# Retention's first state copies in their former order, attention's third group of values split ahead of weights, and the last values copied out of PSUM

## The chip, the core and the metric

The kernel runs on one core of one Trainium2 chip. The metric is the device time of one launch in microseconds (us), as the median of several runs. A core has five engines with queues of their own, each of which runs its instructions in order: TensorE (PE in the profile, with PEld for its weight loads), VectorE (DVE), ScalarE (ACT), GpSimd (POOL) and SyncE (SP, which here only issues transfers). [...]

## The reference

One decoder block on 1024 tokens of width 1024, in float32. Its first sub-layer feeds one normalised input `h` into two mixers whose outputs are gated and added; its second is an MLP.

```python
proj = h @ w_in                                   # q, k, v, gate of both mixers
# retention, 4 heads, 8 chunks of 128 tokens each
s = einsum('bhid,bhjd->bhij', qi, ki) * inner_decay
o = einsum('bhij,bhje->bhie', s, vi) + einsum('bhid,bhde->bhie', qi, state) * q_decay
state = state * chunk_decay + einsum('bhjd,bhje->bhde', ki * k_decay, vi)
# dilated attention, 3 groups (window, dilation) of 4 heads; each gives o and its log-denominator
p = softmax(q k / sqrt(128) + bias);  o = p v
att = einsum('gbhs,gbhsd->bshd', softmax(lse over groups), o_all)
merged = sigmoid(gate_a) * (silu(rg) * groupnorm(ro)) @ w_ret_out + sigmoid(gate_b) * att @ w_att_out
x = x + g1 * (merged @ w_o);   x = x + g2 * (relu(h2 @ w_ff1) ** 2 @ w_ff2)
```

## The kernel before

**Every float32 product is three matmuls.** An operand is split into a high part (`nc.scalar.copy`, ACT, rounding to the matmul's type) and a low part (`nc.vector.tensor_sub`, DVE). `mm3` (line 203) then adds weight-low times input-high (L207), weight-high times input-low (L209) and high times high (L211) in one PSUM bank. So each operand of a matmul costs an ACT instruction and a DVE instruction ahead of it, and TensorE reads both halves.

**The order is written by hand.** There is no scheduler: each engine gets its instructions in the order in which the Python code emits them. `Steps` runs a list of steps; each step has loads (weights of 512 KB into three `raw` buffers, from SP) and a body. The call `ahead(...)` (in other steps `args[0](...)`) inside a body splits the weights of the following steps and prepares their other loads at that place. `weave` and `weave_pv` mix two sources of matmuls on TensorE: a projection (`proj_gen`, eight rounds of six matmuls) and another piece of work; `at(gen, n, call)` calls a function after round `n` of a projection. Where several are nested, the inner one calls first.

**Retention** is done by `chunk(h, c, ...)` (line 706), 32 times; `g` is its number. In each chunk TensorE works at a gate projection (`rg`, tile of two banks), cut into pieces by `ks`, and between the pieces at:

- `kv{h}{c}{i}`, two products of `kh`, `kl` with the values, which update the running state: for `g == 0` ACT and DVE copy them into `sh`, `sl` (L734, L735: the split state) and ACT copies them into `st` (L742, L744); afterwards DVE folds them into `st` (L739);
- `s_kt(i)`: the score `sT` and the transposed key `kT` of chunk `i`. ACT copies (L666), DVE adds and multiplies (L667, L668), ACT and DVE split (L669, L670), and the key goes the same way into `kh`, `kl` (L679, L680);
- `o{h}{c}`: the query with the split state, then the score with the values. DVE takes its statistics (L768 to L770), POOL raises to a power (L771), and DVE writes `onm` (L774), which ends the use of that bank;
- `oT`: four transposes of the `onm` of the chunk before.

`jit_qk(i)` splits query and key of chunk `i`: a copy on ACT (L630) and a subtraction on POOL (L631), the latter with nothing else but the power of L771 on its queue. At the end of a chunk ACT and DVE split the state again (L758, L759). All these products are in one ring of four PSUM banks (`ps_s`), so a product waits for the last reader of the bank four allocations before it; the gate projection and the accumulators of attention have a second ring of two double banks (`ps_mm`). In chunk 1 `ahead(2)` splits the gate weights of chunk 2 (L197 on ACT, L198 on DVE) and multiplies one row block of the conditioning matrix (`mod_prep`, L461 and L463 on DVE).

**Attention** goes in two passes, `pair` 0 and 1, over two of the four heads of each group. For each of six combinations, `att_step` projects keys (`ak`) and computes the scores of the combination before. Then `cover_step` projects parts of the gates while the weights of the softmax and the products with the values are done. `pv` works through banks of probabilities: transposes to `pt` (L1434), a split to `pth` (ACT, L1438) and `ptl` (DVE, L1439), then three matmuls for each block, of `pth` with the low values `vl` (L1458), of `ptl` with the high values `vh` (L1459) and of `pth` with `vh` (L1460). `v_split(pair, g)` (line 1339) makes `vh` from the loaded values (two ACT copies, L1343) and leaves the low part in place of the loaded tile (two DVE subtractions, L1350). Its tiles come from a ring of eight in SBUF.

`pv_end` (line 1462) adds the accumulator `pv{pair}{g}{a}` to the sum of the groups. For group 2 and head `a = 0`, ACT copies the accumulator to SBUF (L1473) and DVE adds it from there (L1476); for `a = 1`, DVE adds it straight from PSUM. Then ACT and DVE split the sum into `ah`, `al` (L1481, L1482), which feed the output projection `ao` (`att_out_step`).

The third group of values of pair 0 is used in the first step of pair 1 (`att_step(1, 0)`), where the key projection `ak` is woven with `pv(0, 2)`; that of pair 1 in `gate_step`, which is woven with `pv(1, 1, 2)` and followed by `att_out_step`.

Of the kernel before, what the change touches and what calls it, by code (L numbers as in the profile page):

```python
# [17 lines left out]
P = 128  # L18
D = 1024
S = 1024  # L20
NK = D // P
# [119 lines left out]
def block_kernel(ctx, tc, io, stop=None, dbg=None):  # L141
    nc = tc.nc
# [354 lines left out]
    def at(gen, n, call):  # L497

        for i, _ in enumerate(gen):
            if i == n:  # L500
                call()
            yield
# [203 lines left out]
    def chunk(h, c, ahead, w=None):  # L706
        p = R["p"]
        g = NC * h + c
        if g + 3 < NG:
            fetch(g + 3)  # L710
        if c % 2 == 0:
            hd["rgw"] = w
            hd["rgp"] = ps_mm(f"rg{h}{c}")

        ks = {0: (5, 6, 6), 1: (6, 7, 8)}.get(g) or [4 * (c % 2) + i for i in (0, 2, 4)]
        if g == 0:
            proj_mm(hd["rgp"], hd["rgw"], range(2))
            s_kt(0)
            proj_mm(hd["rgp"], hd["rgw"], range(2, 5))
        vh, vl = hd["v", g][:, 0], hd["v", g][:, 1]  # L720
        st, sh, sl = R["state"], R["sh"], R["sl"]
        kvs = []
        if c < NC - 1:
            kh, kl = hd["k", g]
            for i in range(2):
                kv = ps_s(f"kv{h}{c}{i}")
                mm3([kv], (kh[:, i, :], kl[:, i, :]), [(vh, vl)], True, True)
                kvs.append(kv)
        if g == 0:
            s_kt(1)  # L730
        proj_mm(hd["rgp"], hd["rgw"], range(*ks[:2]))
        for i, kv in enumerate(kvs):
            if g == 0:
                nc.scalar.copy(sh[:, i, :], kv)  # L734
                nc.vector.tensor_sub(sl[:, i, :], kv, fv(sh[:, i, :]))  # L735
            elif c == 0:
                nc.vector.tensor_copy(st[:, i, :], kv)
            else:
                nc.vector.scalar_tensor_tensor(st[:, i, :], st[:, i, :], float(GAMMA[h] ** C), kv,  # L739
                                               op0=ALU.mult, op1=ALU.add)  # L740
        if g == 0:
            nc.scalar.copy(st[:, 0, :], kvs[0])  # L742
            jit_qk(2)
            nc.scalar.copy(st[:, 1, :], kvs[1])  # L744
        if g == 1:
            s_kt(2)
        ahead(2)
        if 1 < g < NG - 1:
            s_kt(g + 1)
        po = ps_s(f"o{h}{c}")  # L750
        if c > 0:
            t = hd["j", g]
            for i in range(2):
                mm3([po], (t[:, 0, i, :], t[:, 1, i, :]), [(sh[:, i, :], sl[:, i, :])], i == 0, False)
        mm3([po], hd["s", g], [(vh, vl)], c == 0, True)
        if g > 0 and c < NC - 1:
            for i in range(2):
                nc.scalar.copy(sh[:, i, :], st[:, i, :])  # L758
                nc.vector.tensor_sub(sl[:, i, :], st[:, i, :], fv(sh[:, i, :]))  # L759
        if 0 < g < NG - 2:  # L760
            jit_qk(g + 2)
        if g > 0:
            on_T(*divmod(g - 1, NC))
        proj_mm(hd["rgp"], hd["rgw"], range(*ks[1:]))
        bn = p.tile([P, 6], F32, tag="bn", bufs=2, name=f"bn{h}{c}")
        ba = p.tile([P, 2], F32, tag="ba", bufs=2, name=f"ba{h}{c}")
        gr = p.tile([P, 1], F32, tag="gr", bufs=2, name=f"gr{h}{c}")
        nc.vector.bn_stats(bn, po)  # L768
        nc.vector.bn_aggr(ba, bn)
        nc.vector.tensor_scalar(gr, ba[:, 1:2], ct[:, CS_QD2 + h:CS_QD2 + h + 1], GN_EPS, op0=ALU.mult, op1=ALU.add)  # L770
        nc.gpsimd.tensor_tensor(gr, gr, mhalf[:, 0:1], op=ALU.pow)  # L771
        nc.vector.tensor_mul(gr, gr, ct[:, CS_QD + h:CS_QD + h + 1])
        on = p.tile([P, DV], F32, tag="on", bufs=1, name=f"onm{h}{c}")
        nc.vector.tensor_scalar(on, po, ba[:, 0:1], gr, op0=ALU.subtract, op1=ALU.mult)  # L774
        hd["o", h, c] = on
        if c % 2 == 1:
            hd["srg", h, c // 2] = etile(f"srg{h}{c // 2}")
            nc.scalar.activation(hd["srg", h, c // 2], flat(hd["rgp"]), AF.Silu)
        if h > 0 and c < 4:
            u_final(h - 1, (c,))  # L780
# [681 lines left out]
    def pv_end(pair, g, a, acc):  # L1462

        f = flat(acc)
        sumt = A["P", 0, a][:, :1024]
        if g == 0:
            nc.scalar.copy(sumt, f)
        else:

            t = f  # L1470
            if (g, a) != (2, 1):
                t = A["P", g, a][:, :1024]
                nc.scalar.copy(t, f)  # L1473
            r = 4 * g
            sv = sumt.rearrange("p (i r) -> p r i", r=r)
            nc.vector.tensor_add(sv, t.rearrange("p (r i) -> p r i", r=r), sv)  # L1476
        if g == 2:
            h = 2 * pair + a
            ah = A["r1"].tile([P, S], F32R, tag="att", bufs=8, name=f"ah{h}")
            al = A["r1"].tile([P, S], F32R, tag="att", bufs=8, name=f"al{h}")  # L1480
            nc.scalar.copy(ah, sumt)  # L1481
            nc.vector.tensor_sub(al, sumt, fv(ah))  # L1482
            A["att", h] = (ah, al)
# [43 lines left out]
    def att_step(pair, i):  # L1527

        g, a = combos[i]

        def body(*args):
            ps = ps_mm(f"ak{pair}{i}")
            gen = with_sums(proj_gen(ps, args[-1]))
            if i == len(combos) - 2:
                v_fetch(pair, 0)
            if i > 0:
                last = combos[i - 1]
                weave(gen, NK, scores_gen(pair, *last), len(SB[last[0]]), lag=2)
            elif pair == 0:
                args[0](1, True)  # L1540
                for _ in range(4):
                    next(gen)
                on_T(H - 1, NC - 1)
                drain(gen)
                u_final(H - 1)
                for h in range(H):
                    sums_left.extend(sums_of(h))
                open_att()
                args[0](3)
            else:  # L1550

                gen = at(at(gen, 0, lambda: v_split(0, 2)), NK - 1, lambda: k_split(pair, g, a, ps))
                weave_pv(gen, NK - 1, 0, 2)
            if i == 0:
                A["st"] = A["p"].tile([P, 3, 8, 4], F32, tag="st", name=f"st{pair}")
                bias_load(pair)
            if i > 0 or pair == 0:
                k_split(pair, g, a, ps)
            if i > 0:
                scores_end(pair, *last)  # L1560
                if last[1] == 1:
                    stats_out(pair, last[0])
        return body

    def cover_step(pair, n):


        i = COVER[pair][n]

        def body(*args):  # L1570
            ps = ps_mm(f"gate0{i}")
            gen = with_sums(proj_gen(ps, args[-1]))
            if n == 0:
                v_fetch(pair, 1)
                weave(gen, 6, scores_gen(pair, *combos[-1]), len(SB[0]), lag=2, rest=False)
                drain(gen)
                v_split(pair, 0, False)
                scores_end(pair, *combos[-1])
                weights(pair)
                for a in range(2):  # L1580
                    pscale(0, a)
            elif n == 1:
                drain(gen)
            elif n == 2:
                v_fetch(pair, 2)

                gen = at(at(gen, 2, lambda: sigmoids(1)), 3, lambda: (args[0](3), v_split(pair, 1)))
                gen = at(gen, 6, sigmoids)
                weave_pv(gen, NK - 1, pair, 0)
                for a in range(2):  # L1590
                    pscale(1, a)
            else:
                gen = at(at(gen, 3, lambda: [pscale(2, a) for a in range(2)]), 4, lambda: args[0](1))
                gen = at(at(gen, 6, args[0]), 6, sigmoids)
                weave_pv(gen, NK - 1, pair, 1)
            if n > 1:
                t = A["r1"].tile([P, S], F32, tag="att", bufs=8, name=f"g0{i}s")
            else:
                t = ring(f"g0{i}s", F32)
            if n < 3:  # L1600
                nc.vector.tensor_copy(t[:, :512], ps[:, 0])
                nc.scalar.copy(t[:, 512:], ps[:, 1])
                raw_gates.append((i, t))
            else:
                nc.scalar.activation(t, flat(ps), AF.Sigmoid)
                nc.sync.dma_start(gate_d[i], t)
        return body
# [929 lines left out]
```

## Time and profile before

| | us |
|---|---|
| median of three runs | 2215.79 |
| lowest and highest of them | 2214.69, 2216.92 |
| the profiled execution | 2214.59 |
| its span on the core | 2212.7 |

| engine | busy us | share of the span | instructions |
|---|---|---|---|
| PE | 2174.2 | 98% | 10130 |
| PEld | 1803.3 | 81% | 10130 |
| DVE | 1458.7 | 66% | 2289 |
| ACT | 916.7 | 41% | 1679 |
| POOL | 161.1 | 7% | 192 |

The profile is one execution. In the timeline, a row gives the start, the duration, the engine, the line, the operation, output and inputs by tile name, how many like instructions the row merges (`x2`), and in brackets how long the engine sat idle before it and what released it. Retention lies at 657 to 977 us, attention from there to about 1300 us; the three places of the change are near 667, 1115 and 1130, and 1277 us.

### The profile page before, as it was taken

Reading aid. Unit: us, or ns where it says so; the run is one execution under the profiler, and the core shown is the slowest. Engines: PE = TensorE matmul, PEld = TensorE weight load, DVE = VectorE, ACT = ScalarE, POOL = GpSimd, SP = SyncE. Lnnn points to the kernel's source line nnn. Section 1 sums busy time; section 2 is a strip of 40 time slices with the busy share of each in tenths; the row PEclk is TensorE's granted clock in tenths of the full one; section 3 lists DMA queues with packets and bytes.
Section 4 is the critical chain, followed back from the end, with each engine's and each line's share of the span. In section 5 each row is a group of like instructions: output and inputs, shape, how many; then the busy total and the mean of one; then the engine's idle time right before and its main releaser. Section 6 shows DMA issues by size and latency. Waiting matters only on the chain.

```text
span 2212.7 us, 27236 instructions
## 1 busy us (share of the span) xinstructions
PE 2174.2 (98%) x10130; PEld 1803.3 (81%) x10130; DVE 1458.7 (66%) x2289; ACT 916.7 (41%) x1679; POOL 161.1 (7%) x192
## 2 busy tenths in 40 slices
PE   7999999999999999999999999999999999999998
PEld 5888888888887888888888888888778888788887
DVE  6618777764547778865564754676876665787855
ACT  4323332223334445444644634524454445533412
POOL 0001110000012122111100000002000000000003
PEclk9999999999999999999999999999999999999999
DMA  9639999625775556557763265654244444745322
GB/s 366 201 133 281 295 293 289 195 111 181 240 269 189 167 180 216 182 164 195 185 173 96 88 246 182 238 181 162 67 157 152 147 146 182 254 135 175 118 86 77
DMA packets 156611, 408.93 MB, mean 185 GB/s; under 512 B 27446, under 2 KB 55357, under 8 KB 153278
## 3 DMA queue, kind: packets, MB, share of 16 engines
q1 hardware_dynamic: 148542, 363.14, 46.6%
q0 software_dynamic: 7936, 44.05, 9.2%
q8 instruction: 80, 1.31, 0.2%
q14 instruction: 53, 0.43, 0.1%
HBM read 316.27 MB, written 156.13 MB: 213 GB/s over the span
## 4 chain that ended last, share of the span: by engine, by line
PE 60%; DVE 5%; ACT 2%; issue 1%; DMA 1%; POOL 0%; POOLq 0%; SPq 0%; DVEq 0%; ACTq 0%
PE fp L207 4%; PE fp L209 4%; PE fp L211 4%; PE rg L207 2%; PE rg L209 2%; PE rg L211 2%; PE f2a L209 2%; PE f2a L211 2%; PE f2a L207 2%; PE ak L207 2%; PE ak L209 2%; PE ak L211 2%; PE wo L207 1%; PE wo L211 1%; PE wo L209 1%; PE roa L209 1%
## 5 line engine op out<-in xcount | busy, mean ns | idle before, releaser
L207 PE MATMUL qap<-hh,qaw 128*128 128x512 f32 x216 | 84.0, 389 | 0.0
L209 PE MATMUL qap<-hl,qaw 128*128 128x512 f32 x216 | 84.0, 389 | 0.0
L211 PE MATMUL qap<-hh,qaw 128*128 128x512 f32 x216 | 84.0, 389 | 0.0
L631 POOL TENSOR_TENSOR j<-qk,j 128x512 fp32r<-128x512 f32 x32 | 43.7, 1367 | 459.6 <-ACT j L630 440.9
L1996 ACT ACTIVATE a<-a 128x512 f32<-128x512 f32 x48 | 30.3, 632 | 76.1 <-DVE a L1995 76.1
L1893 POOL TENSOR_TENSOR accnf<-accnf,sqnf 128x256 f32<-128x256 f32 (+1 forms) x18 | 16.6, 921 | 613.5 <-ACT sqnf L1892 613.5
L264 DVE TENSOR_TENSOR fw<-w1r,fw 128x512 fp32r<-128x512 f32 x48 | 33.0, 688 | 37.5 <-ACT fw L254 37.5
L1314 ACT ACTIVATE P<-P,ng 128x128 f32<-128x128 f32 (+1 forms) x96 | 41.9, 438 | 37.3 <-DVE ng L1311 37.3
L264 DVE TENSOR_TENSOR qaw<-wa,qaw 128x512 fp32r<-128x512 f32 x54 | 36.0, 685 | 30.6 <-ACT qaw L254 30.6
L2182 ACT CAST w2h<-w2s 128x512 fp32r<-128x512 f32 x36 | 22.4, 622 | 80.3 <-DVE w2s L2220 79.2
L207 PE MATMUL fp<-h2h,fw 128*128 128x512 f32 x128 | 50.0, 391 | 0.0
L211 PE MATMUL fp<-h2h,fw 128*128 128x512 f32 x128 | 49.8, 389 | 0.0
L209 PE MATMUL fp<-h2l,fw 128*128 128x512 f32 x128 | 49.8, 389 | 0.0
L207 PE MATMUL roa<-rh,rwl 128*128 128x512 f32 x128 | 49.8, 389 | 0.0
L209 PE MATMUL roa<-rl,rwh 128*128 128x512 f32 x128 | 49.8, 389 | 0.0
L211 PE MATMUL roa<-rh,rwh 128*128 128x512 f32 x128 | 49.8, 389 | 0.0
L1731 DVE TENSOR_TENSOR rwl<-rwl,rwh 128x1024 fp32r<-128x1024 f32 x25 | 30.2, 1221 | 29.0 <-ACT rwh L1761 29.0
L666 ACT COPY sm<-sT 128x128 f32<-128x128 f32 x32 | 8.5, 265 | 96.5 <-PE sT L654 96.5
L211 PEld LDWEIGHTS qap<-hh,qaw 128*128 128x128 f32 x216 | 40.5, 188 | 8.4
L207 PEld LDWEIGHTS qap<-hh,qaw 128*128 128x128 f32 x216 | 40.6, 188 | 8.4
L209 PEld LDWEIGHTS qap<-hl,qaw 128*128 128x128 f32 x216 | 40.6, 188 | 8.3
L1893 POOL TENSOR_TENSOR accn<-accn,sqn 128x512 f32<-128x512 f32 x12 | 15.5, 1292 | 391.8 <-ACT sqn L1892 391.8
(3099 smaller groups left out, 7210.6 us busy)
## 6 DMA issues: line engine op xcount, KB each, us to landing
v<-vd SPq DMA_DIRECT2D x32, 512.0 KB, 4.7
raw<-in_w_ada_dram SPq DMA_DIRECT2D x32, 512.0 KB, 4.9
w1r<-in_w_ff_dram SPq DMA_DIRECT2D x32, 512.0 KB, 4.9
vd<-vo SPq DMA_DIRECT2D x24, 512.0 KB, 6.2
yt<-y POOLq DMA_DIRECT2D x24, 512.0 KB, 6.9
xsd<-as SPq DMA_DIRECT2D x24, 512.0 KB, 2.7
w2r<-in_w_ff2s_dram SPq DMA_DIRECT2D x24, 512.0 KB, 7.4
em<-in_w_ada_dram SPq DMA_DIRECT2D x16, 512.0 KB, 10.2
```

Source lines behind the costliest of these rows:

```text
L207: nc.tensor.matmul(o, wl, xh, start=first, stop=False, skip_group_check=skip)
L209: nc.tensor.matmul(o, wh, xl, start=False, stop=False, skip_group_check=skip)
L211: nc.tensor.matmul(o, wh, xh, start=False, stop=last, skip_group_check=skip)
L264: nc.vector.tensor_sub(t[:, 512:], src, fv(t[:, :512]))
L631: nc.gpsimd.tensor_sub(t[:, 1], src, fv(t[:, 0]))
L666: nc.scalar.copy(sm, ps[:, :C])
L1314: nc.scalar.activation(v, v, AF.Exp, bias=ng[:, blk:blk + 1], accum_out=st[:, g, blk, 2 + a:3 + a])
L1731: nc.vector.tensor_sub(lo, fv(lo), fv(hi))
L1893: (nc.vector if f == 7 else nc.gpsimd).tensor_add(G["acc", key], G["acc", key], sq)
L1996: nc.scalar.activation(o, o, AF.Relu)
L2182: nc.scalar.copy(hi, src)
```

## The change

Three edits:

1. **Retention, chunks 0 and 1.** In chunk 0, the two copies of the products into `st` move on ACT's queue from ahead of and behind `jit_qk(2)`'s copy to behind it, both of them. In chunk 1, `s_kt(2)` moves behind `ahead(2)`, as in all later chunks: its copies and splits on ACT and DVE come after the split of the gate weights and the conditioning product, and no longer ahead of them. TensorE, POOL and SP keep their order of instructions.
2. **Third group of values, pair 0.** `v_split` moves from round 0 of `att_step(1, 0)` to round 6 of the last `cover_step` of pair 0, ahead of the call that splits the next step's weights. On ACT, two copies go from behind the first `pth` of that group to ahead of `raw_8741h`, two sigmoids, a query's split and `raw_9294h`; on DVE, the two subtractions go from behind the first `ptl` to ahead of `raw_8741l`, the query's low part and `raw_9294l`. TensorE and SP keep their order; the ring hands out the tiles in another order.
3. **`pv_end`.** The accumulator of group 2, head `a = 1`, is copied to SBUF by ACT and added from there by DVE, as for the other head: one ACT instruction more in each pair, and the DVE addition has its input in SBUF and not in PSUM.

```diff
@@ chunk
         if g == 0:
-            nc.scalar.copy(st[:, 0, :], kvs[0])
             jit_qk(2)
-            nc.scalar.copy(st[:, 1, :], kvs[1])
-        if g == 1:
-            s_kt(2)
         ahead(2)
-        if 1 < g < NG - 1:
+        if 0 < g < NG - 1:
             s_kt(g + 1)
         po = ps_s(f"o{h}{c}")
...
         mm3([po], hd["s", g], [(vh, vl)], c == 0, True)
+        for i in range(2) if g == 0 else ():
+            nc.scalar.copy(st[:, i, :], kvs[i])
         if g > 0 and c < NC - 1:
@@ pv_end
-            t = f
-            if (g, a) != (2, 1):
-                t = A["P", g, a][:, :1024]
-                nc.scalar.copy(t, f)
+            t = A["P", g, a][:, :1024]
+            nc.scalar.copy(t, f)
@@ att_step
-                gen = at(at(gen, 0, lambda: v_split(0, 2)), NK - 1, lambda: k_split(pair, g, a, ps))
+                gen = at(gen, NK - 1, lambda: k_split(pair, g, a, ps))
@@ cover_step
-                gen = at(at(gen, 6, args[0]), 6, sigmoids)
+                gen = at(at(at(gen, 6, lambda: v_split(pair, 2)), 6, args[0]), 6, sigmoids)
```

## The prediction

> **What bounds the kernel now.** I read the page first (TensorE is busy nearly throughout), then the timeline of TensorE for its idle brackets, since only a stretch in which TensorE stands still can be won, and at each of those near the change the timelines of the other engines.
>
> ```profile
> PE 2174.2 (98%) x10130; PEld 1803.3 (81%) x10130; DVE 1458.7 (66%) x2289; ACT 916.7 (41%) x1679; POOL 161.1 (7%) x192
> ```
>
> TensorE in retention's chunks 1 and 2, and its granted clock in a stretch (the number before the DMA share):
>
> ```profile
> 671.11 0.44 PE L659 MATMUL kT<-ct,qk 128*128 128x128 f32 x2 [0.75 <-DVE onm L774]
> 671.70 0.51 PE L207 MATMUL o<-stateh,j 128*128 128x512 f32 x1 [0.16 <-DVE state L739]
> ...
> 674.79 0.63 PE L209 MATMUL rg<-hl,raw_4676h 128*128 128x512 f32 x2
> 675.26 0.62 PE L211 MATMUL rg<-hh,raw_4676h 128*128 128x512 f32 x2
> 675.71 0.40 PE L207 MATMUL kv<-v,kl 128*128 128x512 f32 x1
> ...
> 680.16 0.22 PE L654 MATMUL sT<-j 128*128 128x128 f32 x1
> 682.05 0.44 PE L659 MATMUL kT<-ct,qk 128*128 128x128 f32 x2 [1.68 <-DVE onm L774]
> 682.65 0.50 PE L207 MATMUL o<-stateh,j 128*128 128x512 f32 x1 [0.15 <-DVE state L739]
> ...
> 687.32 0.63 PE L209 MATMUL rg<-hl,raw_4763h 128*128 128x512 f32 x2
> ```
>
> ```profile
> 683.40:685.00 1.60, 1.60 (x5) 0.56 0.00 0
> ```
>
> Chunk 1 has 0.91 us of waits, chunk 2 has 1.83, all for the `onm` of the chunk before (whose bank `kT` reuses) and the state update right behind it on DVE. The second is followed by a clock of 0.56: from `o` to the second product of the next `rg`, chunk 1 takes 674.79 - 671.70 = 3.09 and chunk 2, with the same instructions, 687.32 - 682.65 = 4.67, so 1.58 more.
>
> In attention, TensorE waits at all three points that edits 2 and 3 touch:
>
> ```profile
> 1122.59 0.33 PE L1458 MATMUL pv<-pth020(0, 0, 0)_9387,vl 128*128 128x128 f32 x1 [0.71 <-DVE vl L1350]
> 1122.75 0.28 PE L1459 MATMUL pv<-ptl020(0, 0, 0)_9388,vh 128*128 128x128 f32 x1
> ...
> 1136.31 0.72 PE L207 MATMUL ak<-hh,raw_8741l 128*128 128x512 f32 x2 [0.73 <-DVE P L1476]
> ...
> 1279.73 0.73 PE L207 MATMUL ao<-ah,raw_10002l 128*128 128x512 f32 x2 [1.27 <-DVE P L1476]
> ```
>
> **Edit 1, retention.** TensorE's order stays; what moves is when ACT, POOL and DVE deliver. ACT and POOL in chunk 0, then DVE in chunk 1 from the state update to the statistics:
>
> ```profile
> 666.99 0.59 ACT L742 COPY state<-kv 128x512 f32<-128x512 f32 x1 [0.27 <-DVE statel L735]
> 667.47 0.62 ACT L630 CAST j<-qk 128x512 fp32r<-128x512 f32 x1
> ```
>
> ```profile
> 669.43 0.58 POOL L771 TENSOR_TENSOR gr<-gr,ct 128x1 f32<-128x1 f32 x1
> 676.05 1.90 POOL L631 TENSOR_TENSOR j<-qk,j 128x512 fp32r<-128x512 f32 x1 [6.04 <-ACT j L630]
> ```
>
> ```profile
> 670.97 1.28 DVE L739 SCALAR_TENSOR_TENSOR state<-state,kv 128x512 f32<-128x512 f32 x2
> 672.16 0.28 DVE L667 TENSOR_TENSOR sm<-sm,sT 128x128 f32<-128x128 f32 x1
> 672.48 0.29 DVE L668 TENSOR_TENSOR sm<-sm,decay 128x128 f32<-128x128 f32 x1
> 673.13 0.29 DVE L670 TENSOR_TENSOR sml<-sm,smh 128x128 fp32r<-128x128 f32 x1 [0.37 <-ACT smh L669]
> 673.51 0.48 DVE L680 SCALAR_TENSOR_TENSOR kl<-kT,ct,kh 128x256 fp32r<-128x256 f32 x1
> 674.45 1.23 DVE L198 TENSOR_TENSOR raw_4763l<-raw,raw_4763h 128x1024 fp32r<-128x1024 f32 x1 [0.46 <-ACT raw_4763h L197]
> 675.59 1.22 DVE L461 SCALAR_TENSOR_TENSOR raw<-raw,cb 128x1024 f32<-128x1024 f32 x1
> 676.74 0.08 DVE L461 DVE_READ_ACCUMULATOR raw<-raw,cb 128x1 f32 x1
> 676.85 1.12 DVE L463 TENSOR_TENSOR mods<-mods,vec 128x1 f32<-128x1 f32 x1
> 677.90 1.28 DVE L759 TENSOR_TENSOR statel<-state,stateh 128x512 fp32r<-128x512 f32 x2
> 679.10 0.69 DVE L768 BATCH_NORM_STATS2 bn<-o 128x6 f32<-128x512 f32 x1
> ```
>
> *Chunk 0.* The state copy waits 0.27 and takes 0.48 until `j` can follow (667.47 - 666.99); without it ahead, `j` runs at 667.47 - 0.75, about 666.7. On POOL the low part of `j` stands ahead of the power that `onm` needs, and the power follows it without a gap, so both and `onm` come 0.73 earlier. The price: the first state copy, now behind `j`, ends at 667.8 and not 667.58, and the second `kv` of chunk 1, which waits for its bank, starts 0.24 later; the 0.91 of waits behind it takes that up. Chunk 1's `kT` then finds its bank free at 670.4 with no wait, and `o` starts when the first half of the state is out, 670.97 and not 671.70: 0.73 won.
>
> *Chunk 1.* From the state update (now 670.24) DVE does `raw_4763l` at 671.4 (its high part is ready, ACT having been free from 668.3), the conditioning product at 672.6 and its addition at 673.8. That addition took 1.12 in the row, until POOL's `j` (676.05 + 1.90) was through; now POOL is idle then, and I take 0.1, as to the next row after the read of the accumulator. So `sm` starts at 673.9 and not 672.16, and by the rows' spacings `kl` ends at 673.9 + 1.83 = 675.75. The next `kv` needs `kl`: TensorE, 0.73 ahead, waits 0.8 and starts at 675.8, 0.1 later than before. This new wait eats the first gain.
>
> But the large instructions now lie in DVE's wait for scores and no longer behind them: `statel` follows `kl` at once (675.75 to 677.0), the statistics start at 677.0 and not 679.10, and `onm`, which ended at 682.0 (the `kT` at 682.05 was waiting for it), ends 2.1 earlier, at 679.9. TensorE is through with `sT` (680.16 + 0.2) at 680.4, so `kT` no longer waits and `o` starts at 680.55, when the state's first half is out: 2.1 before 682.65. With no wait, the clock has nothing to fall for: 1.58 more. Bounds: if POOL's `j` takes 1.9 and not 1.4 again, 0.5 less; if the clock falls elsewhere, 1.6 less. Edit 1: -3.7, bounds -1.6 and -3.8. From chunk 3 on TensorE has no wait in retention, so nothing there swallows the gain, and the two `raw` buffers come free 2 to 3 earlier, so SP's loads are issued earlier too.
>
> [...]
>
> **Edit 2, values.** ACT and DVE around the wait:
>
> ```profile
> 1118.30 1.04 ACT L197 CAST raw_9294h<-raw 128x1024 fp32r<-128x1024 f32 x1
> 1119.23 0.59 ACT L1438 CAST pth020(0, 0, 0)_9387<-pt020(0, 0, 0)_9382 128x512 fp32r<-128x512 f32 x1
> 1119.71 2.01 ACT L1343 CAST vh<-vl 128x1024 fp32r<-128x1024 f32 x2
> ```
>
> ```profile
> 1119.58 1.22 DVE L198 TENSOR_TENSOR raw_9294l<-raw,raw_9294h 128x1024 fp32r<-128x1024 f32 x1
> 1120.71 0.68 DVE L1439 TENSOR_TENSOR ptl020(0, 0, 0)_9388<-pt020(0, 0, 0)_9382,pth020(0, 0, 0)_9387 128x512 fp32r<-128x512 f32 x1
> 1121.31 2.35 DVE L1350 TENSOR_TENSOR vl<-vl,vh 128x1024 fp32r<-128x1024 f32 x2
> ```
>
> Having the values earlier doesn't end the wait, since ACT has no gap from the accumulator's copy at 1113.6 to 1122: two copies of 0.95 each (2.01 for the pair, overlapping) move ahead, so everything between is 1.9 later. `vl` is ready long before, but `pth` comes at 1121.1 and `ptl`, behind `raw_9294l` which follows its ACT copy, at 1122.6 to 1123.3. The second matmul, L1459, needs `ptl`: 1123.33 and not 1122.75. TensorE loses 0.6. Bounds: 0.9 won if `ptl` is not late, 1.9 lost if the whole shift shows; I take the value between them that `ptl`'s row gives. SP's loads into the three buffers that these splits free are issued some 2 later; their contents are split only after 1137, and 14 us of `ak` and `pv` lie between.
>
> **Edit 3, accumulators.** ACT copies the accumulator (1.0) in the 3.22 us in which it stands idle for DVE (bracket below), so the copy itself costs nothing, and the bank is free 1.0 after the last `pv` matmul and not after DVE has added it. The addition keeps its place on DVE; from SBUF I take it as long as from PSUM, or up to 0.15 longer. TensorE can start 0.16 before the record of the matmul ahead ends (L1459 follows 0.16 after L1458, whose record lasts 0.33), so without a wait it starts at the row's start less bracket less 0.16. *Pair 0:* `ak` would start at 1136.31 - 0.89 = 1135.4; with edit 2's 0.6 it starts at 1136.0 and not 1136.31. `kl` on DVE stands behind the whole chain from `pv` over the additions, comes 0.7 later than before by it and so costs the first scores an estimated 0.2. Edits 2 and 3 here: -0.2, bounds -0.9 and +0.6. *Pair 1:*
>
> ```profile
> 1279.71 1.05 ACT L1481 CAST ah<-P 128x1024 fp32r<-128x1024 f32 x1 [3.22 <-DVE P L1476]
> 1280.66 1.02 ACT L1643 ACTIVATE g<-gate 128x1024 f32<-128x1024 f32 x1
> ```
>
> `ao` starts at 1279.73 - 1.43 = 1278.3. Its second tile, six pairs of 0.45 later (1281.0), needs the bank of the gate projection, which ACT frees behind `ah`: 1280.66 + 1.02 and 0.1 for the longer addition, so 1281.8, as late as before. What is late next is thus ACT's `g`, and its new wait of 0.8 takes back half of the 1.4: -0.6, bounds -1.4 (no such wait) and 0.
>
> Sum: -3.7 - 0.2 - 0.6 = -4.5. The profiled execution took 2214.59, 1.2 less than the median 2215.79; I subtract from the median: 2211.3. A measurement tells 0.2% (4.4 us) from no change, and this lies at that edge.
>
> **Rivals.** *The clock doesn't pay.* If the half clock was this execution's alone, or moves to the new wait of 0.8 at `kv`: -2.9, 2212.9. For it: waits of 1.27 (1279.73) left the clock alone, so a fall hangs on more than the wait. Chance 0.14. *The second wait in retention stays,* if DVE's addition is held by POOL again or the statistics wait for something else: edit 1 gives +0.2, in all -0.6, 2215.2. Against it: the order on DVE. Chance 0.08. *`ptl` is not late:* ACT finds time, edit 2 gains: -5.4, 2210.4. Against it: no gap on ACT in the rows. Chance 0.08. *Slower:* in chunk 1 the weight split and the conditioning product now stand ahead of the scores on ACT and DVE. If they wait, for a load or for a buffer, all behind waits, and TensorE at `kv` with it, us for us, with the half clock (1.6) on top. With w us of such a wait the sum is -2.9 + w: it turns slower from 2.9 on and reaches 0.2% at 7.3, about 2220.5. Against it: in chunk 1 neither instruction shows a wait for a transfer, and they come only 3 us earlier. Chance 0.10.
>
> **Numbers.** The forecast has 0.60, its own range 2210.2 to 2212.3, of which 0.46 is beyond 0.2%. Faster: 0.46 + 0.08 = 0.54; same: 0.14 + 0.14 + 0.08 = 0.36; slower 0.10. The range, 2209.4 to 2215.4, takes in all but the slower case; its low end has edit 2 and the second tile of `ao` at their good bounds.
>
> **What would show it.** Right: in chunk 1 a wait of about 0.8 at `kv` for `kl`, none of 1.68 at the next `kT`, no clock below 1 there; at 1120 (less 3.7) L1459 waiting for `ptl`; no wait at `ak`; the wait at `ao` on its second tile, for ACT's `g`. Wrong: `onm` of chunk 1 still late, a half clock in another place, or a wait in chunk 2 or 3 that is not in the rows above.

## The result and the profile after

The changed kernel takes **2211.7 us** (median of 20 runs, 2210.29 to 2213.4). The kernel before, run beside it, takes 2214.74 (20 runs, 2212.87 to 2218.8). The ratio is 0.9986, with a 95% interval of 0.998 to 0.9992: 3.0 us or 0.14% faster, which is under the 0.2% that the prediction gave as the least that a measurement can tell. In a second comparison (below) the same kernel was 2.4 faster. The profiled execution took 2210.58 (span 2208.7), 4.0 less than the profiled one of before.

TensorE of the changed kernel around the first part of the change (timeline: start, duration, engine, line, operation, and in brackets the idle time ahead and who ended it):

```profile
667.85 0.50 PE L207 MATMUL kv<-v,kl 128*128 128x512 f32 x1 [0.72 <-ACT state L753]
670.43 0.40 PE L659 MATMUL kT<-ct,qk 128*128 128x128 f32 x2
670.91 0.50 PE L207 MATMUL o<-stateh,j 128*128 128x512 f32 x1
...
675.73 0.50 PE L207 MATMUL kv<-v,kl 128*128 128x512 f32 x1 [0.64 <-DVE kl L680]
...
680.35 0.40 PE L659 MATMUL kT<-ct,qk 128*128 128x128 f32 x2
680.51 0.48 PE L207 MATMUL o<-stateh,j 128*128 128x512 f32 x1
...
683.58 0.63 PE L209 MATMUL rg<-hl,raw_4763h 128*128 128x512 f32 x2
```

Neither `kT` waits any more; a new wait of 0.64 for `kl` stands at `kv`. The first `kv` row, which waited 0.33 before, now waits 0.72 for the state copies, as the prediction had it. The last row stood at 687.32. Here is VectorE in the same chunk:

```profile
670.17 1.27 DVE L739 SCALAR_TENSOR_TENSOR state<-state,kv 128x512 f32<-128x512 f32 x2
671.37 1.22 DVE L198 TENSOR_TENSOR raw_4763l<-raw,raw_4763h 128x1024 fp32r<-128x1024 f32 x1
672.50 1.22 DVE L461 SCALAR_TENSOR_TENSOR raw<-raw,cb 128x1024 f32<-128x1024 f32 x1
673.65 0.08 DVE L461 DVE_READ_ACCUMULATOR raw<-raw,cb 128x1 f32 x1
673.76 0.16 DVE L463 TENSOR_TENSOR mods<-mods,vec 128x1 f32<-128x1 f32 x1
673.84 0.28 DVE L667 TENSOR_TENSOR sm<-sm,sT 128x128 f32<-128x128 f32 x1
...
675.19 0.48 DVE L680 SCALAR_TENSOR_TENSOR kl<-kT,ct,kh 128x256 fp32r<-128x256 f32 x1
675.70 1.29 DVE L757 TENSOR_TENSOR statel<-state,stateh 128x512 fp32r<-128x512 f32 x2
676.91 0.69 DVE L766 BATCH_NORM_STATS2 bn<-o 128x6 f32<-128x512 f32 x1
...
679.00 0.81 DVE L772 TENSOR_SCALAR onm<-o,ba,gr 128x512 f32<-128x512 f32 x1
```

The large instructions (1.22 each) now stand ahead of the scores, and the statistics start at 676.91, not 679.10. In attention, TensorE at the points that the other two parts touch:

```profile
1119.63 0.33 PE L1457 MATMUL pv<-ptl020(0, 0, 0)_9394,vh 128*128 128x128 f32 x1 [1.25 <-DVE ptl020(0, 0, 0)_9394 L1437]
...
1132.34 0.62 PE L207 MATMUL ak<-hh,raw_8741l 128*128 128x512 f32 x2
...
1136.87 0.39 PE L209 MATMUL sc<-kl,qh 128*128 128x256 f32 x1 [0.18 <-DVE kl L1259]
...
1278.20 0.73 PE L207 MATMUL ao<-ah,raw_10003l 128*128 128x512 f32 x2 [0.73 <-ACT g L1639]
```

The wait at `pv` has moved from the first matmul (0.71, for `vl`) to the second (1.25, for `ptl`); `ak` no longer waits, the scores wait 0.18; the first tile of `ao` no longer waits, its second tile (this row) waits 0.73 for the gate's sigmoid.

So the steps came nearly as forecast, and this pair of profiles is 4.0 apart. Yet the medians are 3.0 apart. The experiments ask where the rest of the forecast 4.5 went.

### The profile page after: what moved, and what is told of

The parts are those of the page before. It is cut to its first block, busy times and chain, and to the rows that moved or that the text cites. A ratio compares the mean times of both kernels' runs of the same rounds, so it can differ in the third digit from the quotient of the medians.

```text
span 2208.7 us, 27236 instructions
## 1 busy us (share of the span) xinstructions
PE 2172.4 (98%) x10130; PEld 1801.4 (82%) x10130; DVE 1457.4 (66%) x2289; ACT 919.0 (42%) x1681; POOL 160.5 (7%) x192
```

## The experiments

Here "half clock" means a stretch in which the profile shows a granted clock of 0.50. Theory: the sum of the prediction (3.7 for retention with its half clock, 0.8 for attention). Rival: the half clock follows the wait in some executions only. A difference of medians has an interval of some 2 us on either side here, so each reading rests on the profiles too.

**Retention's part alone.**

```diff
         if g == 0:
-            nc.scalar.copy(st[:, 0, :], kvs[0])
             jit_qk(2)
-            nc.scalar.copy(st[:, 1, :], kvs[1])
-        if g == 1:
-            s_kt(2)
+            for i in range(2):
+                nc.scalar.copy(st[:, i, :], kvs[i])
         ahead(2)
-        if 1 < g < NG - 1:
+        if 0 < g < NG - 1:
```

> Retention's part alone (the two state copies of chunk 0 behind its split, and the third group's load of chunk 1 behind the split). Theory: the whole gain of retention is here, two waits of 0.75 and 1.68 us go, one of 0.64 at kv for kl comes, and the half clock (1.58) goes with the second: 3.6 us under the kernel before where its execution has the half clock. Rival: the half clock follows that wait in some executions only; then the medians differ by 2.0 to 3.6 (0.75 + 1.68 - 0.64 = 1.8 from the waits alone). Second rival, the three parts don't add up: less than 1.8.

Measured: 2212.28 against 2214.39, 2.1 less (ratio 0.999, 0.9981 to 0.9999). That is the low end of the rival's range, but the interval (0.2 to 4.2) takes in the theory too. In its profile, `j` waits for a load that the changed kernel's profile didn't show:

```profile
667.26 0.62 ACT L630 CAST j<-qk 128x512 fp32r<-128x512 f32 x1 [0.46 <-DMA qk<-qkd]
```

**Values alone, and accumulators alone** (the third and fourth hunk of the change, and its second).

> The move of the third group of values alone. Theory: the wait of 0.71 at the first pv matmul goes and one of about 1.25 comes at the second, for ptl: 0.5 to 0.6 slower than before. Rival: ptl isn't late here, 0.7 faster. In the profile the half clock of chunk 2 in retention should be there again, as retention is untouched (a further draw on the rival that it comes and goes).

> The copy of the last accumulators alone. Theory: at ak the wait of 0.73 goes and the first scores wait some 0.2 for kl: 0.7 faster there; at the last ao the wait of 1.27 goes and its second tile waits 0.73 for the gate's sigmoid: 0.6 faster; 1.3 in all. Rival: the longer chain copy, addition on DVE delays kl and ah by as much as the bank comes earlier: no gain.

Measured: values 2215.03, 0.6 more (1.0003, 0.9994 to 1.0012); accumulators 2212.38, 2.0 less (0.9991, 0.9982 to 0.9999). The waits in attention are those expected (1.25 at `pv` in the first; none at `ak` and 0.71 for `g` at `ao` in the second). Retention is untouched in both, so both have the wait of 1.68 to 1.70 in chunk 2. Neither has the half clock behind it, which the expectation had put there. This is TensorE of the kernel with the values alone:

```profile
682.26 0.44 PE L659 MATMUL kT<-ct,qk 128*128 128x128 f32 x2 [1.70 <-DVE onm L774]
...
685.95 0.63 PE L209 MATMUL rg<-hl,raw_4763h 128*128 128x512 f32 x2
```

From `kT` to `rg` it takes 3.69, where the kernel before took 5.27 (682.05 to 687.32) in its profile: 1.58 apart, with the same instructions and the same wait but for 0.02. The half clock, then, comes and goes from one execution to the next.

**Both without the values.**

> Retention's part and the accumulators' copy, without the move of the values. Theory: the parts add, 3.6 + 1.3 = 4.9 under before, and 0.5 to 0.6 under the changed kernel, so about 2210.0 on a chip where before takes 2214.8 (3.2 under before where before has no half clock). Rival: the wait of 0.71 at the first pv grows when TensorE comes earlier, and the two kernels are alike.

Measured: 2211.21, 3.2 less than before (0.9984, 0.9976 to 0.9993), so no gain from moving the values shows. Here the load is later still, and this row of its profile shows it:

```profile
668.05 0.62 ACT L630 CAST j<-qk 128x512 fp32r<-128x512 f32 x1 [0.99 <-DMA qk<-qkd]
```

**The two halves of retention's part.** The order of chunk 0's copies alone, and the place of the third group's transposes alone (the first and the last lines of the diff above).

> Of retention's part only the order of chunk 0's state copies. Theory: the wait of 0.75 before chunk 1's kT goes (as far as the load of qk for the next chunk has landed when j wants to start: with j ahead it was waited for 0.46 and 0.99 us in two executions), the 1.68 in chunk 2 stays and is followed by a half clock or not: 0.3 to 0.7 under before. Rival: the two orders only act together, no gain.

> Of retention's part only the third group's transposes and load of chunk 1 moved behind the weight split. Theory: the wait of 0.75 stays, kv of the next chunk waits some 0.6 to 1.4 for kl (the large splits now stand ahead of it on DVE), and the 1.68 goes with its half clock (0.41 of executions, 1.58 us): 1.0 to 1.7 under before. Rival: the new wait at kv is as long as the one removed, no gain but the clock's.

Measured: copies 2214.61, no gain (1.0002, 0.9993 to 1.0011); transposes 2212.24, 2.3 less (0.999, 0.9981 to 0.9999). The stretch on TensorE that holds all these waits, from the first product of chunk 0's `o` (665.57 in the profile of before) to `rg<-hl` behind chunk 2's `o` (687.32), in every profile but that of the longer wait below:

```
edit in retention         stretch, us    j waits for its load   half clock in it
none (before)                 21.75           -                 yes
none (values alone)           20.20           -                 no
none (accumulators alone)     20.16           -                 no
copies only                   21.29           0.30              yes
transposes only               18.83           -                 no
transposes only (2nd)         18.84           -                 no
both (changed kernel)         18.18           -                 no
both (changed, 2nd)           18.20           0.16              no
both (four other kernels)     18.34 to 18.64  0.27 to 0.58      no
both (without the values)     19.04           0.99              no
```

Without the half clock the whole part is worth 2.0 (20.18 to 18.18) when the load has landed, 1.5 to 1.8 with the usual wait for it and 1.1 at its worst. The transposes alone are worth 1.35. The copies add up to 0.65, and less than nothing when the load is at its latest (19.04 against 18.83): `j` then waits 0.99 for its data, and the copies behind it in ACT's queue wait with it (they start at 668.57, and at 667.22 in the changed kernel's first profile).

**What brings the half clock.** The kernel before with chunk 1's statistics taken four times:

```diff
-        nc.vector.bn_stats(bn, po)
+        for _ in range(4 if g == 1 else 1):
+            nc.vector.bn_stats(bn, po)
```

The theory's step is that of the half clock of before (683.59 to 687.00). In the step ahead of it TensorE was busy for 1.58 of 3.41; behind steps with 1.71 (values alone) and 1.84 (accumulators alone) there was none.

> The kernel before with chunk 1's statistics taken four times, so that the wait of 1.68 in chunk 2 becomes 3.6 to 3.8 us. Theory (the clock is set in steps of 3.41 us, and a step in which TensorE stood still for more than half, 1.71, is followed by one at half clock): whatever its place among the steps, this wait has more than 1.71 in one of them, so the half clock follows in every execution: 2.0 for the wait and 0.6 x 1.58 = 0.9 for the executions that had none, 2.9 over before. Rival (the half clock was chance, or a matter of a single wait's length): 2.0 over before, or 3.6.

Measured: 2218.04 against 2214.57, 3.5 more (1.0017, 1.0008 to 1.0026). In its profile, the wait in chunk 2 is this one:

```profile
684.33 0.69 PE L659 MATMUL kT<-ct,qk 128*128 128x128 f32 x2 [3.90 <-DVE onm L775]
```

The wait grew by 2.2, to 3.90, so the theory gives 3.1 (2.2 + 0.9) and the rivals 2.2 or 3.8; the medians can't part these. The windows tell more. Wherever the granted clock falls inside a launch in these profiles (its end left aside), it falls for 3.41 us, and the falls of a launch lie on a grid of such steps: here they begin at 684.13 and 1592.07, 907.94 or 266 times 3.413 apart, and in the kernel before at 683.59 and, at its end, 2205.94, 1522.35 or 446 times 3.413 apart. So busy time can be read step by step. Below, for four kernels, a step and the step behind it: from:to, length, busy time of PE (instructions), PEld, DVE, ACT, POOL, then the granted clock, DMA share and GB/s. The kernel before:

```profile
680.18:683.59 3.41, 1.58 (x8) 1.07 (x8) 2.64 (x6) 0.27 (x1) 0.55 (x1) 1.00 0.68 242
683.59:687.00 3.41, 3.41 (x12) 2.72 (x11) 2.87 (x9) 1.91 (x5) 0.00 (x0) 0.50 0.38 98
```

The kernel with the values alone:

```profile
678.85:682.26 3.41, 1.71 (x11) 1.36 (x9) 2.56 (x7) 0.58 (x2) 0.56 (x1) 1.00 0.97 329
682.27:685.68 3.41, 3.25 (x16) 2.56 (x17) 2.98 (x8) 0.39 (x2) 0.00 (x0) 1.00 0.16 61
```

The kernel with the longer wait:

```profile
680.71:684.12 3.41, 0.00 (x0) 0.00 (x0) 2.53 (x6) 0.02 (x1) 0.56 (x1) 1.00 0.53 193
684.13:687.54 3.41, 3.21 (x8) 2.45 (x9) 3.13 (x8) 0.18 (x1) 0.00 (x0) 0.50 0.00 0
1588.66:1592.07 3.41, 1.71 (x6) 0.74 (x5) 3.34 (x6) 1.50 (x3) 0.00 (x0) 1.00 0.00 0
1592.08:1595.48 3.40, 2.95 (x7) 2.37 (x8) 3.33 (x6) 1.07 (x2) 0.00 (x0) 0.50 0.00 0
```

TensorE busy for 1.58 of 3.41, or not at all: half clock in the next step. Busy for 1.71: once with and once without. The first 25 and the last 20 us of the launch left aside, every step that was busy for 1.66 or less was followed by a fall in the fourteen profiles, and none that was busy for 1.84 or more, but for one in each of the next two. In these profiles, then, what counts is how much of a wait lies in one step, and that depends on where the steps happen to lie. Laying the grid over chunk 2 of before in all positions, 0.41 of them put at least 1.71 us of idle time into one step (an estimate from the timeline's idle times; 1.71 lies between 3.41 - 1.84 = 1.57 and 3.41 - 1.66 = 1.75). The experiment's own profile thus shows the half clock behind a step without any work. The mean granted clock of each run is on record too: with the longer wait it is 0.996 in seven of eleven runs and 0.997 in the other four, and in the kernel before, beside it, 0.996 in one of 33. So the longer wait does bring more half clock. How often it comes with the shorter wait, these means can't tell, since falls at other places and the end of the launch count in them.

**The changed kernel again, and with other banks.** Beside a second comparison, a variant in which the second and the third tile of the last `ao` lie in free single banks, so neither needs the gate's bank:

```diff
-            pss = [ps_mm(f"ao{j}{f}") for f in range(2)]
+            pss = [[ps_s(f"ao{j}{f}{i}") for i in range(2)] if j + f == 1 else ps_mm(f"ao{j}{f}") for f in range(2)]
...
+                if isinstance(ps, list):
+                    for i in range(2):
+                        b = m[:, 512 * i:512 * i + 512]
+                        nc.vector.tensor_mul(b, b, ps[i])
+                    continue
                 nc.vector.tensor_mul(m, m, flat(ps))
```

> The changed kernel, a second time, on the chip of the next three. Theory (retention's gain is 2.0 us of waits less what j waits for the load of qk, 0 to 1.0, plus 1.6 of half clock in some 4 of 10 executions of the kernel before; attention's is 0.65): 2.6 to 3.2 under before in the medians, not 4.5. Rival (the half clock always follows the wait of 1.68): 4.0 to 4.5.

> The changed kernel, with the second and third tile of the last ao in single banks that are free, so that neither needs the bank of the gate's projection early. Theory: the wait of 0.73 for ACT's sigmoid at the second tile goes and nothing comes in its place: 0.7 under the changed kernel. Rival: the tile waits for ah or al of the last head instead, no gain.

Measured: 2212.35 and 2211.1 beside 2214.75 of before (0.999, 0.9981 to 0.9999; 0.9984, 0.9975 to 0.9993). The variant has no wait at any tile of the last `ao`, where the first profile of the changed kernel has 0.73, so what the tile waited for was the bank that ACT's sigmoid reads last. Both profiles have a half clock where the first profile of the changed kernel had none, behind the new wait at `pv`. The changed kernel's second profile:

```profile
1119.57 0.33 PE L1457 MATMUL pv<-ptl020(0, 0, 0)_9394,vh 128*128 128x128 f32 x1 [1.25 <-DVE ptl020(0, 0, 0)_9394 L1437]
...
1125.69 0.22 PE L1456 MATMUL pv<-pth020(4, 0, 4)_9408,vl 128*128 128x128 f32 x1
```

```profile
1118.21:1121.62 3.41, 2.16 (x16) 1.92 (x16) 2.50 (x4) 0.70 (x2) 0.00 (x0) 1.00 0.87 327
1121.63:1125.03 3.40, 3.40 (x12) 2.73 (x11) 0.48 (x1) 0.59 (x1) 0.00 (x0) 0.50 1.02 392
```

It takes 6.12 from the waiting product to the next group, and 4.55 in the first profile (1119.63 to 1124.18): 1.57 lost again. The first profile, with the same wait:

```profile
1116.39:1119.80 3.41, 2.16 (x13) 1.50 (x11) 3.25 (x5) 2.58 (x5) 0.84 (x1) 1.00 0.48 90
1119.81:1123.20 3.39, 3.39 (x23) 3.03 (x24) 0.96 (x2) 0.21 (x1) 0.00 (x0) 1.00 1.03 376
```

TensorE is busy for 2.16 in both steps, more than the 1.84 above, so busy time alone doesn't part them. In the step with the fall behind it, most of the work is `pv` products of 128 columns. Those start 0.11 apart (nine from 1119.79 to 1120.80 in the first profile), against 0.23 for 512 columns (four from 1121.42 to 1122.35), so they move half as many columns per us; counted by columns (an estimate), this step is some 0.4 busy. In the first profile the step holds wide products ahead of the wait and is near half by that count. That columns are what counts isn't shown: it rests on these profiles alone. Of four profiles with this wait, two have the half clock. The 20 times of the changed kernel lie in two heaps of ten, up to 2211.41 and from 2211.99 up, and their mean granted clock is 0.999 in four of the lower ten and in none of the upper, which fits; that the heaps are these two cases isn't shown.

**A version without the new waits.** Retention's part and the accumulators' copy; the values left where they were, but the next step's splits called two rounds later, behind the transposes (`at(..., 2, args[0])`, with that step marked "late"); and a free bank pair for the second tile of `ao`, in a first form for this tile alone:

> Retention's part and the accumulators' copy, values left where they were, and two changes against the new waits: at attention's step with the third group of values the next step's splits come behind two of its transposes (so vl, pth and ptl are ready: the 0.71 at pv goes), and the second tile of the last ao goes to two single banks that are free, not to the gate's bank (the 0.73 for the sigmoid goes). Theory: 0.7 and 0.7 under the kernel with those two parts alone, so 4.5 to 4.9 under before and 1.3 to 1.9 under the changed kernel. Rival: the later splits make the next scores or ak late by as much, or the last ao waits for ah in its place.

Measured: 2210.74, 3.8 less than before (0.9984, 0.9975 to 0.9993). The waits at `pv` and `ao` were gone, but the first product behind `ao` now waited for a bank still in use; the likely cause is that an odd number of large banks had been handed out:

```profile
1318.42 0.47 PE L207 MATMUL roa<-rh,rwl 128*128 128x512 f32 x1 [1.41 <-DVE g L1698]
```

With two tiles moved, as in the diff above, and once more with chunk 0's copies in their order of before:

> Retention's part, the accumulators' copy, the later splits at the third group of values, and the two tiles in free banks. With one tile moved, the first product after ao waited 1.41 us for the last product with the gates, since the order of the two large banks had changed; with two moved it is again as in the changed kernel. Theory: that wait goes, so 1.2 to 1.4 under that kernel: about 2209.5, 5.0 under before, 1.9 under the changed kernel. Rival: another wait takes its place before the next projection, no gain over it.

> As the kernel ahead of it, but with chunk 0's two state copies in their place of before (one ahead of the split, one behind). Theory: the wait of 0.75 at chunk 1's kT is back, the one at the second kv is 0.4 shorter, and the split no longer waits for its load: 0.6 slower at the most, 0.3 faster at the best. Rival: the order of the copies is worth the 0.73 that was put on it.

Measured: **2208.52**, 6.2 less than before (0.9974, 0.9964 to 0.9984), and 2209.23 (0.9976, 0.9967 to 0.9986). With two tiles moved the wait of 1.41 is gone. The first of the two versions beats both kernels: its slowest run took 2208.96, the fastest of the changed kernel beside it 2210.86. It is 3.8 under the changed one, in whose profile 1.25 of wait at `pv`, 1.57 of half clock behind it and 0.65 of wait at `ao` stood, 3.5 in all; none of the three is left. With the half clock in one execution of two (an estimate from the four profiles) the three make 2.7 on average, so some 1 us stays open. Its eight times lie within 0.92 us, those of the changed kernel beside it within 3.49. The order of the copies is worth 0.7 between these two medians, whose intervals overlap.

## Why the prediction was right, and where it was wrong

The time, 2211.7, is 0.4 from the forecast, but that closeness is luck: two errors offset each other. The gain was 3.0 and 2.4 in two comparisons, not 4.5; and the kernel before, by 20 runs, stands at 2214.74, not at the 2215.79 of the three runs from which the sum was subtracted. The gain is that of the rival "the clock doesn't pay" (2.9), which had 0.14 and whose first condition, a half clock of "this execution's alone", is nearest to what the runs showed. "Faster by over 0.2%" had most of the chance, and the measured 0.14% is "same".

*Chunk 0 and chunk 1: right.* `j` at 666.69 (forecast 666.7), `o` at 670.91 (670.97), `kv` after a wait of 0.64 at 675.73 (0.8, 675.8), DVE's addition 0.16 long once POOL's `j` is out of its way (0.1), statistics at 676.91 (677.0), `onm` finished at 679.8 (679.9), `o` of chunk 2 at 680.51 (680.55). This execution began the stretch 0.17 ahead of the profile of before (665.40, 665.57), so each step is up to 0.2 later than it looks. That the first gain is eaten by the wait for `kl`, and the second comes from the statistics, also holds: alone, the copies showed no gain and the transposes gave most.

*"With no wait, the clock has nothing to fall for: 1.58 more": the step that failed.* Its size was right (1.58 from `kT` to `rg`, with and without), but it was counted in full, from one execution. It is there in some executions only: in two of the four profiles with the wait of 1.68 to 1.70. By the estimate of 0.41 it is worth some 0.65 on average, 0.9 less than counted.

*Edit 2, and the clock again.* The second matmul came 0.62 later against its surroundings (1119.63, where 1122.75 less the 3.74 already won is 1119.01), forecast 0.6. What the prediction didn't see is that this new wait, too, is followed by a half clock in some executions. It had the rival that the fall "moves to the new wait", but at `kv`, whose 0.64 never brought one. With 1.57 in two of four profiles, edit 2 gives back about as much of the clock (0.8, an estimate) as edit 1 wins.

*The load, another mis-sized term.* `j` at 666.7 took for granted that its data lie ready. In the profile of before, the load of `qk` was issued at 657.89 and landed 8.74 later, at 666.63, so there was next to no margin; over the fourteen profiles it took 8.7 to 9.8, and that of before was the quickest. The prediction had a load that comes late as its slower rival, in chunk 1; it comes in chunk 0, and costs 0.3 on average, all of the 0.73 at its worst: `j` waited 0.16 to 0.99 in seven of eight profiles that have it ahead of the copy, and the stretch of the seven with both edits was 18.5 on average, not 18.18. With these three terms the sum is 4.5 - 0.9 - 0.8 - 0.3 = 2.5, an estimate beside the measured 3.0 and 2.4.

*Edit 3: right in its steps.* `ak` didn't wait, the scores waited 0.18 (0.2), the second tile of `ao` waited 0.73 for ACT's `g` (0.8). Edits 2 and 3 together moved TensorE from 3.74 to 4.39 ahead, 0.65 (1282.59 in before to 1278.20); forecast 0.8. All of it came in pair 1 (0.7, forecast 0.6). In pair 0 the lead was 3.67 behind the first scores (1140.77 in before, 1137.10), so nothing was won. The forecast 0.2 there is also a slip: by its own terms (0.9 won at `ak`, 0.6 lost at `pv`, 0.2 lost at the scores) it should have been 0.1.

## What to carry to other kernels

An effect that follows a wait in one profile has to be seen in several executions before it is counted in full: here the granted clock fell to 0.50 for steps of 3.41 us, and whether a wait of 1.25 to 1.7 us brought one, at a cost of 1.56 to 1.59, depended on where the steps lay, as far as these profiles show. Such waits fit the spread of the times: 3.1 and 3.5 us for the changed kernel, 0.9 for the version without them. That a single new wait widens the spread isn't shown: the values alone spread over 3.1, the kernel before, beside them, over 3.6. When an instruction is moved ahead, look at when its load lands (here 8.7 to 9.8 us after its issue), and in several executions, and not only at the queue in front of it.

## What was not expected of the hardware

- In these profiles the half clock came in steps of 3.41 us, and whether one came went with TensorE's busy time in the step ahead: at 1.58 of 3.41 yes, at 1.71 once yes and once no, at 1.84 no; with `pv`'s 128-column products in it, at 2.16, twice yes and twice no. It cost 1.56 to 1.59 us in the four profiles in which it fell behind the wait of 1.68 at `kT` or of 1.25 at `pv`, and 1.2 behind the wait of 3.90 (684.33 to 689.20 from `kT` to `rg`, 4.87 against 3.69). Between 1583 and 1592 us, where TensorE waits for VectorE some 1.1 us at a time, it fell in seven of the fourteen profiles; some 25 us behind it, counted from the first `n21ss` ahead of it, these stand at most 0.13 later than the others.
- A VectorE addition of one column took 1.12 us beside POOL's `j` and 0.16 without, and that `j` took 1.90 beside VectorE's large instructions and 1.36 in the changed kernel.
